# Parameters as rows, late gates of the second block, and state space inputs made ahead in a hybrid decoder block

## The chip, the cores and the metric

The kernel runs on one core of a Trainium2 chip. The metric is the device time of one execution in microseconds (us). Each profile is of one execution. The engines are PE (TensorE, with weight loads listed apart as PEld), DVE (VectorE), ACT (ScalarE), POOL (GpSimd) and SP (SyncE, which issues every DMA here, in program order).

## The reference

One decoder layer for 2048 tokens of width 1024, float32 throughout:

```python
h = _rms(x, norm1_g)
u, q, k, v, qi, ki, wi, gates = split(h @ w_in)           # 512, 512, 64, 64, 256, 64, 4, 2048 columns
# state space: 32 groups of 16 channels and 64 complex states
dt = exp(log_dt); abar = exp((A_re + i A_im) * dt)         # per group and state
b = coef(abar, A) * (B @ u)                                # B: 64 x 16 per group
s = associative_scan(abar, b); y = Re(C @ s) + D_skip * u
y = gelu(y); y_ssm = y * sigmoid(y @ w_glu + b_glu)
# attention: each token takes the 256 visible keys of the highest index score
iscore = sum_heads(relu(qi @ ki^T) * wi); idx = top_k(iscore, 256)
y_att = softmax(q @ k[idx]^T / 8) @ v[idx]                 # 8 heads, one shared k and v
g_ssm, g_att = split(gates)                                # 1024 columns each
merged = sigmoid(g_ssm) * (y_ssm @ w_proj_ssm) + sigmoid(g_att) * (y_att @ w_proj_attn)
x = x + merged @ w_out
x = x + (silu(rms(x) @ w_ffn_gate) * (rms(x) @ w_ffn_up)) @ w_ffn_down   # 2816 hidden columns
```

## The kernel before

All large products run with each float32 operand split in a high and a low part: `mm3` issues three matmuls for each 128 rows of the contraction, so a product of 128 columns by 512 tokens over 1024 rows is 24 matmuls. Every instruction goes through one recording function and therefore carries line 206; a group is told by its tiles.

`phase1` makes the RMS norm, turns `x` into `hT` (high and low), and multiplies it by the columns of `w_in` for u, q, k, v, qi, ki and wi, in tiles `mm`. A step loads pieces of `w_in` into `raw`, DVE and POOL split them into `w`, PE multiplies. Beside this the parameters of the state space branch are computed on DVE. `ssm_params` doesn't run them at once: it fills a list `queue` (with `Later`, which notes a call for later), and `phase1` takes items of it one by one between its own steps. First in the list stand the loads of A_re, A_im, log_dt, D_skip, B_re, B_im, then C_re and C_im, then the arithmetic, then `turns`, which turn C on PE. The half of `hT` for each 1024 tokens is also stored to `hTd`.

Then three generators run side by side, and `Pace` writes their steps into one order when the program is built, by its own estimates of when each engine is free. On the chip this order is fixed for each engine.

- `state`: first `ssm`. Its `prepare` makes, mostly on POOL, the matrices of 8 blocks of 4 groups (powers of abar times B and C: `Gr`, `Er`, `K0`, `M`, `F`, the turned `ET`, the phases `pc`; `N0` is how many columns of the phases are made for all blocks at once). Its `solve` turns the block's inputs U into `Ut`, multiplies them by `ET` (`ee`), runs the recurrence on DVE (`z`, `S`) and multiplies by `M` and `F` into `Y`. `gelu` turns Y to `yT`. All their products use one PSUM bank (`sps`), and an ACT copy empties it each time. Then `glu` multiplies by w_glu (tiles `u<-yp,uw`) and stores `act_d`. When it is through, `gated` is set.
- `attention`: four groups of 4 tiles of 128 tokens. For each, `topk` searches the threshold of the 256th score by counting (on DVE `jkd`, on ACT `jka`, with updates `un`, `tr` on DVE); then `attention` makes the logits (`lg`), the turned probabilities (`pt`, split in `th` and `tl`) and the output (`po`), and stores `att_d`.
- `dense`: first `gates`, 64 products `gps<-hT,gw` (32 column tiles times two runs of 512 tokens; ACT's tanh gives `gsg`, which is stored to `gate_d`). The second half of the tokens (`hf` 1) comes first, from `hT` in SBUF; the first half is loaded back from `hTd`. Then it waits for `gated`, and runs four blocks of 512 tokens in `block`: the two branches' projections (192 matmuls `f<-act,ww`), times the gates, into `mg`; `w_out` (384 matmuls `f<-ww,mg` of 256 columns); norm; FFN up (`f<-h,ww`, then silu and the split `at`) and down (`f<-wd,at`). Block `tb` starts when attention group `tb` is through.

Block 0 loads and splits the weights itself (`raw` to `ww` and `wd`, on DVE, POOL and ACT) and stores the split copies `wc`; the later blocks load them, 1 MB each, through rings of buffers (`Rings`). The list of these items is made in `weights`. At the end of a block the next block's branch inputs `act` are loaded (`load_branch`), 2 MB each.

Of the kernel before, what the change touches and what calls it, by code (L numbers as in the profile page):

```python
# [12 lines left out]
F32 = mybir.dt.float32  # L13
# [22 lines left out]
G = 32  # L36
# [329 lines left out]
class Block:  # L366
    def __init__(self, ctx, tc, a, out):
# [24 lines left out]
        self.bias_d = [d.tile([128, (i + 1) * 128], BF16, name=f"bias{i}") for i in range(NT)]  # L392
        self.gate_d = [[d.tile([128, HALF], F32, name=f"gate{j}_{h}") for h in range(2)] for j in range(2 * KD)]
# [341 lines left out]
    def gates(self, hT, st):  # L735
# [37 lines left out]
        left = [2] * (2 * NG)  # L773
        for q, (n, tg) in enumerate(order):
# [9 lines left out]
            if q in (2 * NG - 2, 2 * NG):  # L784
                parts.extend((q - 2 * NG + 2 >> 1, h, i) for h in range(2) for i in range(2))
# [212 lines left out]
    def attention(self, st, tiles, nP, nT, causal):  # L998
# [6 lines left out]
        tp = self.pool(st, "at", 3 if KL <= 1536 else 2, side="right")  # L1005
# [224 lines left out]
    def ssm_params(self, pr, wk, ps_t, queue):  # L1230
# [3 lines left out]
        dv, sync, cmul = Later(queue, nc.vector), Later(queue, nc.sync), self.cmul  # L1234
        sh = [128, NS]
        A = {}
# [4 lines left out]
        dt = wk.tile(sh, F32, name="dt")  # L1241
        ap = a["log_dt"]
        for g2 in range(2):
            sync.dma_start(dt[g2 * 64:(g2 + 1) * 64],
                              bass.AP(tensor=ap.tensor, offset=ap.offset + g2, ap=[[0, 64], [2, NS]]))
        Ds = pr.tile([32, NS], F32, name="Ds")
        ap = a["D_skip"]
        sync.dma_start(Ds, bass.AP(tensor=ap.tensor, offset=ap.offset, ap=[[1, 32], [32, NS]]))
        B, C, turns = [], [], []
        for n in ("B_re", "B_im"):  # L1250
            t = wk.tile([128, NS, PG], F32, name=n)
            ap = a[n]
            sync.dma_start(t, bass.AP(tensor=ap.tensor, offset=ap.offset,
                                         ap=[[PG, 128], [128 * PG, NS], [1, PG]]))
            B.append(t)
        for n in ("C_re", "C_im"):
# [16 lines left out]
        ar, ai = A["A_re"], A["A_im"]  # L1273
# [55 lines left out]
        u1, u2 = (wk.tile([128, NS, PG], F32, name=f"u{n}") for n in "12")  # L1329
# [5 lines left out]
        dv.tensor_tensor(eye, self.ident[:32, 0:PG], self.ident[:32, PG:2 * PG], op=ALU.add)  # L1335
        queue.extend(turns)
        return m8, ap_r, ap_i, wt, Bb, C, eye, Ds

    def ssm(self, st, params):
# [9 lines left out]
        made = deque()  # L1349
        taken = [0]  # L1350
        NS, N0 = G // 2, 32

        def prepare():
# [8 lines left out]
            dd = wk.tile([32, NS, PG], F32, name="dd")  # L1362
            gp.tensor_tensor(dd, eye[:, None, :].to_broadcast([32, NS, PG]), Ds[:, :, None].to_broadcast([32, NS, PG]),
                             op=ALU.mult)
# [6 lines left out]
            for blk in range(NBLK):  # L1371
# [42 lines left out]
                yield self.pace.idle("POOL", K0)  # L1414
                gp.tensor_tensor(K0[:, :, 0], K0[:, :, 0], dd[:, ss], op=ALU.add)
# [8 lines left out]
                ET = wk.tile([128, 2, SB, 128], F32, name="ET", bufs=2)  # L1424
                for i, E in enumerate((Er, Ei)):
                    yield at("PE", E, psp.free_at("sp"), wk.free_at("ET", 2) if i == 0 else 0.0)
                    ps = psp.tile([128, 512], F32, name="sp")
                    for sp in range(SB):
                        nc.tensor.transpose(ps[:, sp * 128:(sp + 1) * 128],
                                            E[:, sp].rearrange("p t c -> p (t c)"), self.ident)  # L1430
                    nc.scalar.copy(ET[:, i].rearrange("p s n -> p (s n)"), ps[:, :SB * 128])
# [21 lines left out]
                made.append((F2, M, ET, pc))  # L1453
# [6 lines left out]

        def solve(blk):
            s0 = blk * SB
            U = Us.popleft()
            yield lambda: at("PE") if made else NEVER
            F2, M, ET, pc = made.popleft()
            Ut = wk.tile([128, GB, 2, 128], F32, name="Ut")
            for g in range(0, GB, 2):
                yield at("PE", U, psp.free_at("sp"))
                ps = psp.tile([128, 512], F32, name="sp")
                for q in range(4):  # L1470
                    nc.tensor.transpose(ps[:, q * 128:(q + 1) * 128], U[:, q % 2, g + q // 2], self.ident)
                nc.scalar.copy(Ut[:, g:g + 2].rearrange("p g a c -> p (g a c)"), ps)
            if blk + 1 < NBLK:
                Us.append(load(blk + 1))

            ee = wk.tile([128, 2, SB, NCH], F32, name="ee")
            e = [ee[:, i] for i in range(2)]
            for sp in range(SB):
                yield at("PE", ET, Ut, psp.free_at("sp"))
                ps = psp.tile([128, 512], F32, name="sp")  # L1480
                for i in range(2):
                    for g2 in range(2):
                        nc.tensor.matmul(ps[g2 * 64:(g2 + 1) * 64, i * 256:(i + 1) * 256],
# [519 lines left out]
```

## Time and profile before

| | us |
|---|---|
| three runs | 3389.36, 3391.08 (median), 3392.07 |
| profiled execution | 3392.47 |
| its span, first to last instruction | 3390.8 |
| granted TensorE clock, mean | 0.972 |

Where the stages lie in the profiled execution, by the first and last instructions of their tiles on PE (for the searches, on DVE):

| stage | us from the start |
|---|---|
| phase 1 | 0 to 366 |
| gates (`gps`) | 366 to 981 |
| state space (`sp`) | 381 to 782 |
| attention 0 | 518 to 740 |
| search 1 | 758 to about 1155 |
| GLU (`u`) | 799 to 901 |
| block 0, projections from | 990 |
| block 0, `w_out` from | 1065 |
| attention 1 | 1163 to 1383 |
| search 2 | 1414 to 1833, block 1 from 1632 |
| attention 2 | 1833 to 2090 |
| search 3 | 2105 to 2520, block 2 from 2268 |
| attention 3 | 2520 to 2896 |
| block 3, alone | 2924 to the end |

A row of the profile for a group names engine, operation, and the tiles it writes and reads. A wait "PE f <- DVE un" says that PE's next product into `f` was released by DVE's work on `un`. Of several waits the one that ended last is named.

### The profile page before, as it was taken

What the parts mean: (1) busy time and instruction counts of PE and PEld (TensorE: products, weight loads), DVE (VectorE), ACT (ScalarE), POOL (GpSimd) and SP (SyncE); (2) the same over time, 40 slices, a digit from 0 to 9 for tenths busy, and PEclk for the clock granted to TensorE, in tenths of its full rate; (3) what the DMA queues carried; (4) which work ended last, traced back from release to release, by engine and by line L of the source; (5) the groups of instructions that cost most, each with busy time, mean ns of one, the idle gap of its engine ahead of it and who ended that gap; (6) DMA issues with size and microseconds to landing.
All of it is one profiled execution on the core that took longest, in us unless ns stands there. A gap on an engine that the chain in (4) does not pass through costs nothing. (4 is left out here: it accounts for less than half of the span.)

```text
span 3390.8 us, 44218 instructions
## 1 busy us (share of the span) xinstructions
PE 3179.1 (94%) x16292; PEld 2687.4 (79%) x16292; DVE 2118.4 (62%) x4540; ACT 1277.2 (38%) x2210; POOL 622.4 (18%) x620
## 2 busy tenths in 40 slices
PE   6999999899878999988889999999999999899999
PEld 5889777677767888876788888878888888698887
DVE  5565595655687767689686675867776666322223
ACT  3141444445552444355412443666124443010000
POOL 3323666522233212134100000000000000000000
PEclk8999999999989999999999999999999999999999
DMA  4834423434458766656845324376472332755554
GB/s 135 249 119 116 132 77 121 153 123 142 130 174 293 271 210 231 238 175 236 310 152 218 146 105 165 123 259 229 166 271 99 114 133 103 271 193 201 204 199 161
DMA packets 321527, 605.67 MB, mean 179 GB/s; under 512 B 52896, under 2 KB 205216, under 8 KB 290592
## 3 DMA queue, kind: packets, MB, share of 16 engines
q1 hardware_dynamic: 321312, 602.86, 51.1%
q8 instruction: 128, 2.10, 0.2%
q14 instruction: 87, 0.71, 0.1%
HBM read 434.71 MB, written 166.89 MB: 177 GB/s over the span
## 5 line engine op out<-in xcount | busy, mean ns | idle before, releaser
L206 PE MATMUL f<-h,ww 128*128 128x512 f32 (+1 forms) x4416 | 1015.0, 384 | 1.4 <-DVE h L206 1.1
L206 PEld LDWEIGHTS f<-h,ww 128*128 128x128 f32 x4416 | 800.6, 190 | 156.4 <-DVE h L206 1.9
L206 PE MATMUL f<-wd,at 128*128 128x512 f32 x2112 | 521.1, 399 | 42.8 <-DVE un L206 16.0
L206 PEld LDWEIGHTS f<-wd,at 128*128 128x128 f32 x2112 | 398.5, 192 | 133.3 <-DVE x L206 13.6
L206 PE MATMUL gps<-hT,gw 128*128 128x512 f32 x1536 | 386.5, 402 | 5.2 <-ACT gsg L206 3.7
L206 ACT ACTIVATE jka<-S,tr 128x1536 bf16<-128x1536 f32 (+5 forms) x217 | 305.6, 1408 | 193.6 <-DVE tr L206 119.2
L206 PEld LDWEIGHTS gps<-hT,gw 128*128 128x128 f32 x1536 | 287.7, 192 | 70.0 <-ACT gsg L206 6.4
L206 DVE TENSOR_TENSOR x<-f,x 128x512 f32<-128x512 f32 x352 | 236.4, 687 | 103.2 <-PE f L206 102.5
L206 PE MATMUL mm<-w,hT 128*128 128x512 f32 (+1 forms) x1152 | 281.5, 402 | 7.2 <-DVE hT L206 7.0
L206 DVE TENSOR_TENSOR tl<-pt,th 128x512 fp32r<-128x512 f32 (+1 forms) x288 | 184.2, 658 | 135.9 <-ACT th L206 135.1
L206 PEld LDWEIGHTS mm<-w,hT 128*128 128x128 f32 x1152 | 241.8, 241 | 32.6 <-DVE hT L206 8.7
L206 DVE SCALAR_TENSOR_TENSOR t<-t,f 128x512 f32<-128x512 f32 (+1 forms) x125 | 83.5, 668 | 278.5 <-PE f L206 238.0
L206 ACT CAST th<-pt 128x512 fp32r<-128x512 f32 (+1 forms) x288 | 155.8, 563 | 234.1 <-PE pt L206 230.3
L206 PE MATMUL f<-act,ww 128*128 128x512 f32 x768 | 189.9, 408 | 29.7 <-POOL ww L206 9.1
L206 PEld LDWEIGHTS f<-act,ww 128*128 128x128 f32 x768 | 149.2, 197 | 70.3 <-POOL ww L206 13.3
L206 PE MATMUL f<-ww,mg 128*128 128x256 f32 x1536 | 190.4, 287 | 10.8 <-ACT ww L206 4.5
L206 PEld LDWEIGHTS f<-ww,mg 128*128 128x128 f32 x1536 | 188.7, 195 | 12.9 <-ACT ww L206 5.0
L206 ACT ACTIVATE P<-P,m 128x1024 f32<-128x1024 f32 (+7 forms) x192 | 172.3, 900 | 54.5 <-DVE m L206 54.4
L206 POOL TENSOR_TENSOR g<-g,g 128x512 f32<-128x512 f32 x31 | 39.8, 1285 | 813.3 <-DVE g L206 793.5
L206 PE MATMUL lg<-kk,q 128*128 128x512 f32 (+1 forms) x640 | 183.7, 388 | 1.1 <-DMA kk<-kk 1.1
L206 ACT ACTIVATE t<-f 128x512 f32<-128x512 f32 (+1 forms) x92 | 53.0, 576 | 332.9 <-PE f L206 332.7
L206 ACT CAST at<-t 128x512 fp32r<-128x512 f32 (+1 forms) x92 | 55.3, 601 | 324.1 <-DVE t L206 324.1
(359 smaller groups left out, 4492.2 us busy)
## 6 DMA issues: line engine op xcount, KB each, us to landing
ww<-wc SPq DMA_DIRECT2D x180, 1024.0 KB, 4.9
wd<-wc SPq DMA_DIRECT2D x66, 1024.0 KB, 8.3
wc<-ww SPq DMA_DIRECT2D x60, 1024.0 KB, 7.7
raw<-in_w_in_dram SPq DMA_DIRECT2D x104, 256.0 KB, 3.4
wc<-wd SPq DMA_DIRECT2D x22, 1024.0 KB, 7.6
x<-in_x_dram SPq DMA_DIRECT2D x32, 512.0 KB, 5.1
gate<-gsg SPq DMA_DIRECT2D x64, 256.0 KB, 2.2
g<-gate SPq DMA_DIRECT2D x64, 256.0 KB, 5.0
```

Of the source, the lines that this page charges most:

```text
L206: return f(*args, **kw)
```

## The change

It has three parts.

1. `ssm_params` loads A_re, A_im, D_skip and log_dt as 16 rows each, of contiguous runs (128, 128, 32 and 2 numbers), instead of number by number into columns, and turns them on PE in one bank (`columns`). Each load of B is cut in four, and these eight stand between the steps of the arithmetic, one after every sixth.
2. The gates of block 1's tokens (16 of the 64 products: first half of the tokens, second run of 512) leave `gates`. The split weights for them are stored as `gw_d`, 16 tiles of 1 MB. At the end of block 0 `load_tokens` loads `hT` of these tokens into the buffers of `act`; `block` makes the 16 products first, then loads the two branches into the same buffers, the attention's first, and takes the branches in that order.
3. In `ssm` the inputs' part of `solve` becomes a generator `enter`, up to one block ahead. Both halves of `ET` take one bank and one copy; `ee` one copy for both parts; `Y` one bank and one copy for each 128 channels, with both pairs of groups in it. The skip D is added on DVE. `N0` is 16, not 32. Apart from these, `th` and `tl` in attention 0 have two buffers, not three.

```diff
@@ gates
-        order = [(n, tg) for n in range(2 * NG) for tg in range(2)]
-        order[2 * NG - 4:2 * NG + 4] = [(NG + n, tg) for n0 in (-2, 0) for tg in range(2) for n in (n0, n0 + 1)]
+        order = [(n, tg) for n in range(NG) for tg in range(2)] + [(NG + n, 0) for n in range(NG)]
+        order[2 * NG - 4:2 * NG] = [(n, tg) for tg in range(2) for n in (NG - 2, NG - 1)]
...
+            if n >= NG:
+                nc.sync.dma_start(self.gw_d[ct], w.rearrange("p z k c -> p z (k c)").bitcast(F32))
@@ ssm_params
-        for n in ("A_re", "A_im"):
-            A[n] = wk.tile(sh, F32, name=n)
-            ap = a[n]
-            sync.dma_start(A[n], bass.AP(tensor=ap.tensor, offset=ap.offset, ap=[[1, 128], [128, NS]]))
...
+        for z, n, m in ((rows[0], "A_re", 128), (rows[1], "A_im", 128), (d32, "D_skip", 32), (d2, "log_dt", 2)):
+            sync.dma_start(z, bass.AP(tensor=a[n].tensor, offset=a[n].offset, ap=[[m, NS], [1, m]]))
...
+            for i, z in enumerate(rows):
+                nc.tensor.transpose(ps[:, i * NS:(i + 1) * NS], z, self.ident[:NS, :NS])
+            nc.tensor.transpose(ps[:32, 3 * NS:4 * NS], d32, self.ident[:NS, :NS])
+            nc.scalar.copy(A.rearrange("p a s -> p (a s)"), ps[:, :3 * NS])
...
-            sync.dma_start(t, bass.AP(tensor=ap.tensor, offset=ap.offset,
-                                         ap=[[PG, 128], [128 * PG, NS], [1, PG]]))
+            for s0 in range(0, NS, 4):
+                sync.dma_start(t[:, s0:s0 + 4], bass.AP(tensor=ap.tensor, offset=ap.offset + s0 * 128 * PG,
+                                                        ap=[[PG, 128], [128 * PG, 4], [1, PG]]))
...
+        queue.extend(head)
+        queue.extend(loads.popleft() for _ in range(24))
+        queue.append(columns)
+        for i, step in enumerate(steps):
+            queue.append(step)
+            if i % 6 == 5 and loads:
+                queue.append(loads.popleft())
@@ ssm
+        def enter():
+            U = load(0)
+            for blk in range(NBLK):
+                yield lambda: at("PE") if turned and len(entered) < 1 else NEVER
...
-                for i in range(2):
-                    nc.scalar.copy(e[i][:, sp], ps[:, i * 256:(i + 1) * 256])
+                    nc.scalar.copy(ee[:, :, sp], ps.rearrange("p (i c) -> p i c", i=2))
...
-        return self.pace.among([apply(), prepare()])
+        return self.pace.among([apply(), enter(), prepare()])
@@ block
+            if tb in self.late:
+                b0 = 1
...
+                    order = list(range(KD))
+                    last = 3
+                    for ct in range(2 * KD - last):
+                        w = ld.get("w")
+                        yield ready(w, *hg)
+                        ps = bank()
+                        yield from products(ps, w, order)
+                        ld.drop("w")
+                        gated(ct, ps)
+                    order = [*range(KD // 2, KD), *range(KD // 2)]
+                    banks = []
+                    for i in range(last):
+                        w = ld.get("w", i)
+                        yield ready(w)
+                        banks.append(bank(False))
+                        yield from products(banks[i], w, order[:KD // 2])
+                    self.act = [None, self.load_branch(bigp, 1, tb)]
+                    for i in range(last):
+                        w = ld.get("w")
+                        yield from products(banks[i], w, order[KD // 2:])
+                        ld.drop("w")
+                        gated(2 * KD - last + i, banks[i])
+                    self.act[0] = self.load_branch(bigp, 0, tb)
```

How the order of instructions changes is shown at three places. The first is SP's queue in phase 1, where the parameters are loaded; `u_577` and `u_578` are the tiles of the rows. Before:

```order
L206 DMA raw<-in_w_in_dram 128x512 x3
L206 DMA A_re<-in_A_re_dram 128x16x1
L206 DMA A_im<-in_A_im_dram 128x16x1
L206 DMA dt<-in_log_dt_dram 64x16x1 x2
L206 DMA Ds<-in_D_skip_dram 32x16x1
L206 DMA B_re<-in_B_re_dram 128x16x16
L206 DMA B_im<-in_B_im_dram 128x16x16
L206 DMA C_re_568<-in_C_re_dram 16x2x64
L206 DMA raw<-in_w_in_dram 128x512 x3
```

Seven loads of parameters and one of C stand between two groups of weight loads. SP's queue at the same place after:

```order
L206 DMA raw<-in_w_in_dram 128x512 x3
L206 DMA u_577<-in_A_re_dram 16x128
L206 DMA u_577<-in_A_im_dram 16x128
L206 DMA u_578<-in_D_skip_dram 16x32
L206 DMA u_578<-in_log_dt_dram 16x2
L206 DMA C_re_584<-in_C_re_dram 16x2x64 x4
L206 DMA raw<-in_w_in_dram 128x512 x3
```

Four loads of rows and four of C stand there, and none of B. The second place is PE at the end of the gates, with the GLU's products `u` and the first products of block 0. Before:

```order
L206 MATMUL gps<-hT,gw 128x512 x24
L206 MATMUL u<-yp,uw_7369 128x256 x12
L206 MATMUL u<-yp,uw_7374 128x256 x12
L206 MATMUL gps<-hT,gw 128x512 x6
L206 MATMUL u<-yp,uw_7416 128x256 x12
L206 MATMUL u<-yp,uw_7443 128x256 x12
L206 MATMUL gps<-hT,gw 128x512 x330
L206 MATMUL f<-act_9327,ww 128x512 x24
```

330 matmuls of gates stand between the GLU's last products and block 0. PE's order at the same place after, with the products `tps` of search 1 among them:

```order
L206 MATMUL gps<-hT,gw 128x512 x24
L206 MATMUL u<-yp,uw_7375 128x256 x12
L206 MATMUL u<-yp,uw_7402 128x256 x12
L206 MATMUL tps<-kis,qi 128x512 x4
L206 MATMUL u<-yp,uw_7327 128x256 x12
L206 MATMUL u<-yp,uw_7332 128x256 x12
L206 MATMUL tps<-kis,qi 128x512 x4
L206 MATMUL tps<-kis,qi 128x256 x8
L206 MATMUL u<-yp,uw_7375 128x256 x12
L206 MATMUL u<-yp,uw_7402 128x256 x12
L206 MATMUL u<-yp,uw_7327 128x256 x12
L206 MATMUL u<-yp,uw_7332 128x256 x12
```

The last gates stand ahead of the last ten GLU groups here (two of them follow these rows), and block 0's first product `f` follows the GLU. The third place is PE from block 0's last products to block 1's first. Before:

```order
L206 MATMUL f<-h_9802,ww 128x512 x12
L206 MATMUL f<-h_9803,ww 128x512 x12
L206 MATMUL f<-wd,at 128x512 x96
L206 MATMUL f<-act_14451,ww 128x512 x24
L206 MATMUL f<-act_14456,ww 128x512 x24
```

Block 1's projections follow block 0's last products. PE's order at the same place after, from the end of the late gates (`hg` are the tokens' tiles; 13 products of 24 matmuls stand ahead of these rows, and ahead of them the last 66 of `f<-wd,at`):

```order
L206 MATMUL f<-hg_13749,ww 128x512 x12
L206 MATMUL f<-hg_13752,ww 128x512 x48
L206 MATMUL f<-hg_13749,ww 128x512 x36
L206 MATMUL f<-act_14727,ww 128x512 x24
L206 MATMUL f<-act_14807,ww 128x512 x24
```

The 384 matmuls of the late gates stand between the last product of block 0 and the projections of block 1; the last three products are taken half by half.

More of the change, by code (lines that the diff above doesn't have):

```diff
@@ L1272, in ssm_params @@
             C.append(t)
-        ar, ai = A["A_re"], A["A_im"]
+        ar, ai = A[:, 0], A[:, 1]
         edt, _ = self.exp_parts(dv, dt, wk, sh, "ed")
@@ L1335, in ssm_params @@
         dv.tensor_tensor(eye, self.ident[:32, 0:PG], self.ident[:32, PG:2 * PG], op=ALU.add)
+        loads.extend(late)
+        queue.extend(head)
[5 more added lines that the diff above has]
+                queue.append(loads.popleft())
+        assert not loads and len(steps) > 7 * 16
         queue.extend(turns)
@@ L1413, in prepare @@
                 nc.scalar.copy(K0.rearrange("p s t c -> p (s t c)"), ps[:32, :SB * 128])
-                yield self.pace.idle("POOL", K0)
-                gp.tensor_tensor(K0[:, :, 0], K0[:, :, 0], dd[:, ss], op=ALU.add)
+                yield at("DVE", K0)
+                for sp in range(SB):
+                    dv.scalar_tensor_tensor(K0[:, sp, 0], eye, Ds[:, s0 + sp:s0 + sp + 1], K0[:, sp, 0], op0=ALU.mult,
+                                            op1=ALU.add)
                 M = Ms[blk % 2]
@@ L1461, in solve @@
         def solve(blk):
             s0 = blk * SB
[L1463 to L1472, printed above, removed]
@@ L1473, in solve @@
-            if blk + 1 < NBLK:
-                Us.append(load(blk + 1))
-            ee = wk.tile([128, 2, SB, NCH], F32, name="ee")
-            e = [ee[:, i] for i in range(2)]
-            for sp in range(SB):
-                yield at("PE", ET, Ut, psp.free_at("sp"))
-                ps = psp.tile([128, 512], F32, name="sp")
-                for i in range(2):
-                    for g2 in range(2):
-                        nc.tensor.matmul(ps[g2 * 64:(g2 + 1) * 64, i * 256:(i + 1) * 256],
-                                         ET[:, i, sp, g2 * 64:(g2 + 1) * 64],
-                                         Ut[:, sp * 2 + g2].rearrange("p a c -> p (a c)"), start=True, stop=True)
-                for i in range(2):
-                    nc.scalar.copy(e[i][:, sp], ps[:, i * 256:(i + 1) * 256])
+            yield lambda: at("PE") if made and entered else NEVER
@@ L1664, in weights @@
         copies = [self.dram.tile([128, 2, 1024], F32, name=f"wc{i}") for i in range(len(items))]
-        return [(kind, parts, copy, tb > 0) for tb in range(NB) for (kind, parts), copy in zip(items, copies)]
+        return [z for tb in range(NB) for z in
+                [("w", None, copy, True) for copy in self.gw_d if tb in self.late] +
+                [(kind, parts, copy, tb > 0) for (kind, parts), copy in zip(items, copies)]]
     def load_branch(self, bigp, br, tb):
@@ L1672, in load_branch, with load_tokens @@
         return z
+    def load_tokens(self, bigp, tb):
+        hg = []
+        for i in range(2):
+            ks = slice(i * KD // 2, (i + 1) * KD // 2)
+            hg.append(bigp.tile([128, 2, KD // 2, TB], F32R, name=f"hg{i}", tag=f"act{i}"))
+            for z in range(2):
+                self.nc.sync.dma_start(hg[i][:, z].bitcast(F32), self.hT_d[:, z, ks, tb * TB:(tb + 1) * TB])
+        return hg
     def block(self, tb, bigp, ld, nps, nd):
@@ L1918, in block @@
             if tb + 1 < NB:
-                self.act = [self.load_branch(bigp, br, tb + 1) for br in range(1 + (self.attended >= 4 * (tb + 2)))]
+                if tb + 1 in self.late:
+                    self.act = self.load_tokens(bigp, tb + 1)
+                else:
+                    self.act = [self.load_branch(bigp, br, tb + 1)
+                                for br in range(1 + (self.attended >= 4 * (tb + 2)))]
             yield from down(pairs.popleft(), False)
```

133 lines of the change are left out of this document (90 added, 43 removed).

## The prediction

> **What bounds the kernel now.** I read the page's busy times first, then a table of windows cut at the stages, then the waits of TensorE (PE) inside each stage, and last the timelines at the waits that the change touches.
>
> ```profile
> PE 3179.1 (94%) x16292; PEld 2687.4 (79%) x16292; DVE 2118.4 (62%) x4540; ACT 1277.2 (38%) x2210; POOL 622.4 (18%) x620
> ```
>
> PE is busy for 3179.1 of a span of 3390.8 us and no other engine is above 62%. The change keeps the matmuls (the late gates are the same products in another place), so only the 211.7 us in which PE idles, and stretches at a low clock, can move. Where they lie, by stage (columns: length; busy time of PE, PEld, DVE, ACT, POOL; granted clock; DMA share; GB/s):
>
> ```profile
> 366.00:758.00 392.00, 360.98 (x1796) 285.45 (x1797) 256.56 (x586) 185.17 (x413) 230.04 (x348) 0.94 0.38 118
> 758.00:1163.00 405.00, 352.43 (x1888) 298.77 (x1887) 282.31 (x664) 188.34 (x318) 104.45 (x70) 0.95 0.58 191
> 1163.00:1414.00 251.00, 249.80 (x1324) 211.47 (x1323) 166.53 (x324) 108.54 (x188) 45.92 (x20) 1.00 0.66 229
> 1414.00:1834.00 420.00, 379.30 (x1837) 317.50 (x1836) 332.63 (x676) 171.39 (x226) 91.90 (x48) 0.95 0.64 231
> 1834.00:2105.00 271.00, 270.12 (x1542) 233.19 (x1540) 181.36 (x399) 121.98 (x254) 0.00 (x0) 1.00 0.36 130
> 2105.00:2520.00 415.00, 393.70 (x1932) 333.00 (x1932) 319.31 (x688) 194.35 (x222) 15.19 (x16) 0.97 0.56 206
> ```
>
> The stages are: state space beside attention 0 (31 us idle), search 1 with the gates, the GLU and the start of block 0 (53), attention 1 (1), search 2 (41), attention 2 (1), search 3 (21). PE idles while a search loads VectorE (DVE), hardly ever in an attention stage.
>
> **Part 1, parameters as rows.** The rows are the one wait of PE between 69 and 92 us, SyncE's (SP's) queue, DVE's and PE's first work after it, and a window behind it.
>
> ```profile
> PE tp L206 <- DVE hT L206: 22.2, 1, 22.2
> ```
> ```profile
> 56.80 0.42 SPq L206 DMA_DIRECT2D A_re<-in_A_re_dram  x1
> 57.28 3.56 SPq L206 DMA_DIRECT2D A_im<-in_A_im_dram  x1
> 60.88 2.57 SPq L206 DMA_DIRECT2D dt<-in_log_dt_dram  x2
> 63.49 3.12 SPq L206 DMA_DIRECT2D Ds<-in_D_skip_dram  x1
> 66.66 4.80 SPq L206 DMA_DIRECT2D B_re<-in_B_re_dram  x1
> 71.50 12.86 SPq L206 DMA_DIRECT2D B_im<-in_B_im_dram  x1
> ...
> 85.81 1.31 SPq L206 DMA_DIRECT2D raw<-in_w_in_dram  x3
> 87.18 3.98 SPq L206 DMA_DIRECT2D C_re<-in_C_re_dram  x8
> ```
> ```profile
> 88.70 0.43 DVE L206 CAST w<-raw 128x512 fp32r<-128x512 f32 x1 [23.31 <-DMA raw<-in_w_in_dram]
> ...
> 91.74 1.97 PE L206 MATMUL tp<-ident,q 128*128 128x128 f32 x8 [22.15 <-DVE hT L206]
> ```
> ```profile
> 91.00:96.00 5.00, 4.26 (x14) 3.76 (x15) 3.58 (x5) 0.10 (x1) 2.98 (x3) 0.50 0.72 221
> ```
>
> Seven element-wise loads stand on SP from 56.80 to 84.36 us. The weight load `raw` stands behind them, DVE idles 23.31 us for it, and PE 22.15 us for DVE; behind that the granted clock is 0.50. In the new order eight short DMAs (four rows, four of C) stand ahead of the same `raw`. Eight such loads of C took 3.98 us, so 4 us stand there instead of 27.6: the queue is shorter by 23.6 us, more than the wait. I take the whole 22.2 us and about 2 us of the half clock (5 us at 0.50 lose 2.5): **−24**, bounds 0 (if the loads of the weights stand behind something else) and −25. Four turns on PE and four copies on ACT are added while PE waits or runs full; like `tp` turns they take under a us, so 0.
>
> The loads of B are cut in eight, not re-formed: their runs stay 64 bytes long. In the rows they hold SP for 4.80 + 12.86 = 17.66 us, so 2.2 us a piece, issued one between each six steps of DVE, with `raw` loads between them. A wait of 2.2 us spread over products of 24 matmuls can be hidden: 0, bounds 0 and +17.7. The Trainium skill ("DMA: Bandwidth & Descriptors", sections Specifications and Rules for kernel authors) says that an innermost run with stride costs one descriptor per element, and that runs under 512 bytes don't reach line rate. By its measure A, log_dt and D are mended wholly and B not at all, and the sum would be +17.7 worse; the trace agrees as far as the loads with 4-byte and 64-byte runs alone hold SP for more than 2 us.
>
> **Part 2, the state space branch.** It has one PSUM bank (`sps`), so each product waits for the copy of the one before. The waits of PE between 366 and 758 us, and ACT's copies of Y:
>
> ```profile
> PE sp L206 <- DVE z L206: 10.0, 3, 5.7
> PE sp L206 <- ACT Y L206: 8.0, 4, 2.7
> PE sp L206 <- ACT Ut L206: 4.5, 2, 4.3
> PE sp L206 <- ACT ee L206: 4.1, 2, 3.8
> PE sp L206 <- DVE S L206: 1.9, 2, 1.6
> ```
> ```profile
> L206 ACT COPY Y<-sp 128x256 f32<-128x256 f32 x32 | 11.8, 370 | 39.8 <-PE sp L206 37.3 <-issue 2.5
> ```
>
> The sums are 28.5 us in the five first rows. Y goes from four turns of the bank per block to two, with copies twice as wide: of its 8.0 us I take −5. `Ut` and `ee` are made up to a block ahead, when nothing waits for them: of 8.6 us half, −5 with rounding. `z` and `S` are the recurrence itself, 0. Sum **−10**. Bounds: −28.5, if `z` waited because its inputs were late; +8.6, if the new generator holds the one bank when `solve` wants it. The skip's move from POOL to DVE is 16 additions of 32x16 on a DVE with 135 us idle in that stage: 0. Two buffers for `th` and `tl` instead of three in attention 0: of the stage's 31.0 us of idle time all but 2.5 stand in the five rows, so 0, bounds 0 and +2.5 (that rest once more).
>
> **Part 3, the late gates.** Sixteen gate products (384 matmuls) leave search 1 and stand in front of block 1, in search 2. Their length, and what block 0 and block 1 lose under a search:
>
> ```profile
> 990.00:1065.00 75.00, 55.76 (x193) 40.32 (x192) 55.03 (x116) 17.77 (x26) 31.53 (x19) 0.86 0.86 298
> 1065.00:1163.00 98.00, 90.97 (x622) 85.17 (x623) 71.57 (x121) 34.33 (x49) 22.22 (x12) 0.95 0.74 268
> ...
> 3100.00:3200.00 100.00, 100.00 (x443) 82.81 (x442) 24.56 (x36) 7.30 (x12) 0.00 (x0) 1.00 0.52 198
> ```
>
> Undisturbed, a matmul takes 100/443 = 0.226 us, so the late gates are 87 us. Search 1 ends near 1155 us by the marks; its DVE work is not moved, so 87 us more of block 0 now run beside it. Block 0 lost 7.03 of 98 us (7.2%) in its second window: 87 × 7.2% = **+6**. The last GLU groups lose their company too; the waits of this stretch:
>
> ```profile
> PE f L206 <- DMA act<-act: 8.9, 1, 8.9
> PE u L206 <- ACT t L206: 7.9, 7, 2.2
> PE u L206 <- DVE yp L206: 3.8, 5, 1.0
> ```
>
> Twelve GLU waits cost 11.7 us now, 0.98 us each, beside gates; ten groups stand behind the last gate in the new order. Between 0 and +9.8 for them I take **+5**. The 8.9 us for the first branch's load stay, since it follows the GLU in both orders. Bounds of these two terms: 0 and +77 (the rival below, and 9.8).
>
> Search 2 gains what it had lost, as far as gates, which ask DVE for nothing, replace FFN work. PE's waits there:
>
> ```profile
> PE f L206 <- DVE un L206: 10.7, 4, 4.9
> PE f L206 <- DVE x L206: 9.4, 4, 4.7
> ...
> PE f L206 <- DVE t L206: 2.5, 1, 2.5
> ```
>
> These 22.6 us are waits for a DVE behind in its queue. The gates cover 87 of the search's 218 us (1414 to 1632), and block 1's products then meet the rest: half, −11. The branches are loaded late, into the tiles that hold the tokens: the load of the attention's share goes while 36 matmuls (8.1 us) run, and such loads land in some 9 us, so +2 for both. Together **−9**, bounds −22.6 and +9. Storing and loading the split weights is 32 MB more; a load of 1 MB has 87/16 = 5.4 us, or 193 GB/s, and the row of 990:1065 shows 298 GB/s: 0, bounds 0 and +9 (one such load late).
>
> The end: attention 3 now stands further ahead of block 3, whose start waited here (from 2888 to 2960 us):
>
> ```profile
> PE f L206 <- DMA wd<-wc: 6.3, 2, 5.4
> PE f L206 <- DMA act<-att: 3.5, 3, 1.9
> ```
>
> The second row goes, and the first stays: **−4**, bounds −9.8 and 0.
>
> **Sum.** −24 −10 +6 +5 −9 −4 = −36. The profiled execution took 3392.5 us, so 3356.5; it lies 1.4 us above the median of the runs, 3391.1, so **3355**. Less than 0.2% (6.8 us) I call no change.
>
> **The rivals.**
> - *Block 0 under a whole search (slower).* Its first products, 193 matmuls, took 75 us and should take 43.6: 42% lost, with splits on POOL and ACT beside a search on DVE. In the new order block 0 has 165 + 87 = 252 us beside search 1, of which 177 follow the first window. At 42% these lose 74 us, against 7 now: +67 in place of +6, or 3416 us. For it: the splits of weights go on through block 0. Against it: the second window, also beside the search, lost only 7.2%. It decides from a loss of 28% on (177 × 28% = 50 = 7 + 6 + 36).
> - *The stall comes back at B.* Its 17.7 us of SP time fall on loads that PE waits for: 3373 us. For it: 12.86 us for one load of 64-byte runs. Against it: the pieces stand between weight loads that are issued ahead. The rule of the Trainium skill cited above ("DMA: Bandwidth & Descriptors", Rules for kernel authors) speaks for this one.
> - *More is gained than I take.* `z` was late for its inputs, so that all 28.5 us of the branch go, and all 22.6 of search 2: 19 and 13 us more, 3323 us. For it: DVE busy only 65% beside `z`. Against it: the recurrence is a chain, and search 2 ends when DVE does.
> - *The change does less than it says*, as the bank is the bound and not the turns: neither fuller banks nor gates in another place count, and only part 1 does: 3391 − 24 = 3367 us, inside the first case.
>
> **How the numbers follow.** My forecast has 0.50, with a band of its own from 3335 to 3376 (half the way to the bounds of the branch and of search 2, 16 us down and 18 up, and some 3 for the GLU); the larger gain 0.20; the return of the stall 0.16; block 0 under the search 0.14. The range from 3312 to 3392 takes in the first three; its low end is that of the larger gain with the end's and the GLU's bounds, 11 us on. Out of it are most of the slower case and little else. Faster by over 0.2%: 0.50 + 0.20 + nearly all of 0.16, less a little of each for the unknown: 0.80; no change 0.10 (the slower case at about 28% and a stall with small gains); slower 0.10.
>
> **What would show it.** Right: between 55 and 100 us no load on SP but B above 1 us, and no wait of PE above 5 us; waits on `Y`, `Ut` and `ee` under 8 us together; PE idle in the stretch from the GLU's end to search 1's end near 7%; in front of block 1 a stretch of 384 `f` products with hardly a wait, and then waits on `un` and `x` of half their size. Wrong: a wait on `raw` or `w` behind a piece of B; waits of `f` on `ww` from POOL or ACT of 40 us or more in block 0; a wait of 5 us or more on `act` in front of block 1; a new wait of `sp` on a bank held by `Ut`.

## The result and the profile after

The changed kernel takes 3430.7 us (median of 4, 3427.9 to 3431.8) against 3391.6 us before: ratio 1.011, 95% interval 1.0095 to 1.0126, 38 us slower. The forecast was 3355 us, 36 us faster. Of the rivals, block 0 under a whole search (3416 us) had the right sign and place.

The page's first line for the changed kernel shows the same matmuls in a longer span (3429.3 us):

```profile
PE 3186.1 (93%) x16296; PEld 2689.7 (78%) x16296; DVE 2140.7 (62%) x4554; ACT 1270.9 (37%) x2176; POOL 644.5 (19%) x652
```

The windows of the changed kernel at its own stages (columns as before): state space and attention 0; block 0's projections, its `w_out` and norm, its FFN, all three beside search 1; search 2 up to block 0's end; the late gates.

```profile
352.00:757.00 405.00, 365.92 (x1843) 288.71 (x1844) 282.44 (x613) 190.60 (x391) 235.20 (x380) 0.96 0.41 127
...
900.00:976.00 76.00, 55.90 (x193) 41.46 (x193) 54.90 (x122) 33.14 (x53) 33.75 (x19) 0.84 0.85 295
976.00:1062.00 86.00, 53.81 (x401) 52.20 (x401) 75.47 (x176) 42.33 (x71) 45.16 (x22) 0.78 0.52 180
1062.00:1234.00 172.00, 149.15 (x664) 122.00 (x664) 144.70 (x252) 43.20 (x67) 65.05 (x29) 0.93 0.68 238
...
1483.00:1579.00 96.00, 86.00 (x361) 68.78 (x362) 75.76 (x130) 46.05 (x55) 14.54 (x9) 0.93 0.63 229
1579.00:1671.00 92.00, 87.36 (x385) 71.69 (x383) 76.72 (x273) 79.37 (x105) 0.00 (x0) 1.00 0.73 242
```

Block 0 now spends 334 us beside search 1, and PE is busy for 259 of them; in `w_out` and norm it is busy for 54 of 86. The late gates run as meant: their 384 matmuls stand in the last window, of 92 us, which has one more.

To add up losses, idle time and low clock together, I take for each stretch its length less its matmuls at the spacing that they have where nothing is waited for (0.227 us for 512 columns). In us:

| stretch | before | changed | part 1 alone | part 3 alone | part 2 alone | 1 and 3 |
|---|---|---|---|---|---|---|
| to the first gate | 66.0 | 51.2 | 52.3 | 66.6 | 66.2 | 50.8 |
| to the end of attention 0 | 53.8 | 58.9 | 54.7 | 64.4 | 39.1 | 65.6 |
| to block 0's first product | 34.9 | 41.5 | 39.0 | 36.6 | 55.3 | 36.0 |
| block 0 (with attention 1) | 95.7 | 132.3 | 98.2 | 124.9 | 123.0 | 125.9 |
| late gates, block 1's projections | 0.0 | 15.5 | 0.1 | 2.0 | 15.1 | 2.8 |
| from there to block 3 | 86.9 | 80.4 | 80.7 | 77.3 | 86.1 | 76.8 |
| block 3 | 8.4 | 4.1 | 7.9 | 2.5 | 3.1 | 2.1 |
| all | 345.7 | 383.9 | 332.9 | 374.3 | 387.9 | 360.0 |

The four columns on the right are the first experiments. The profiled execution of parts 1 and 3 took 3407.8 us, 8 above the median of its runs, so that its column is some 8 us high. What the changed kernel gains in phase 1 (15) and in the last rows (11) it loses twice over in block 0 (37) and in front of block 1's `w_out` (15).

### The profile page after: what moved, and what is told of

Same layout as the page of the kernel before. It is cut to its first block, busy times and chain, and to the rows that moved or that the text cites. A ratio compares the mean times of both kernels' runs of the same rounds, so it can differ in the third digit from the quotient of the medians.

```text
span 3429.3 us, 44303 instructions
## 1 busy us (share of the span) xinstructions
PE 3186.1 (93%) x16296; PEld 2689.7 (78%) x16296; DVE 2140.7 (62%) x4554; ACT 1270.9 (37%) x2176; POOL 644.5 (19%) x652
## 5 line engine op out<-in xcount | busy, mean ns | idle before, releaser
L206 ACT ACTIVATE jka<-S,tr 128x1536 bf16<-128x1536 f32 (+6 forms) x217 | 305.4, 1407 | 195.3 <-DVE tr L206 112.6
L206 PE MATMUL gps<-hT,gw 128*128 128x512 f32 x1152 | 295.0, 405 | 3.3 <-ACT gw L206 2.0
L206 PEld LDWEIGHTS gps<-hT,gw 128*128 128x128 f32 x1152 | 216.0, 193 | 51.5 <-issue 3.5
L206 ACT CAST at<-t 128x512 fp32r<-128x512 f32 (+1 forms) x92 | 55.3, 601 | 359.6 <-DVE t L206 359.1
```

What stands on the lines that cost most here:

```text
L206: return f(*args, **kw)
```

## The experiments

All ratios are to the kernel before, run on the same chip.

| kernel | median, us | ratio, 95% interval |
|---|---|---|
| part 1 alone | 3380.3 | 0.9955 (0.9942 to 0.9969) |
| part 3 alone | 3419.6 | 1.0076 (1.0062 to 1.0089) |
| parts 1 and 3 | 3400.0 | 1.0023 (1.0013 to 1.0032) |
| part 2 alone | 3433.5 | 1.0119 (1.0105 to 1.0133) |
| before, no splits | 3346.2 | 0.9863 (0.9847 to 0.9880) |
| changed, no splits | 3374.7 | 0.9948 (0.9933 to 0.9963) |
| part 3, no splits | 3347.9 | 0.9867 (0.9853 to 0.9882) |
| changed, block 0's splits without POOL | 3401.0 | 1.0027 (1.0014 to 1.0040) |
| part 1, the same | 3372.5 | 0.9945 (0.9933 to 0.9958) |
| parts 1 and 3, the same | 3379.5 | 0.9956 (0.9944 to 0.9969) |
| changed, half the late gates | 3437.2 | 1.0130 (1.0117 to 1.0143) |
| part 2, gates inside block 0 | 3439.2 | 1.0132 (1.0117 to 1.0146) |
| part 1, splits without POOL, idle POOL operations | 3438.8 | 1.0135 (1.0122 to 1.0149) |
| part 3 without the lead | 3392.9 | 1.0001 (0.9990 to 1.0011) |
| part 1, no split on POOL after phase 1 | 3363.3 | 0.9909 (0.9896 to 0.9923) |
| changed, no branch loads in block 1 | 3422.2 | 1.0086 (1.0069 to 1.0102) |
| the fastest, with part 3 without lead | 3387.6 | 0.9987 (0.9978 to 0.9996) |
| changed, no split on POOL after phase 1 | 3409.5 | 1.0057 (1.0045 to 1.0070) |

**Each part alone.** My first theory after the result was that the late gates do all the harm (lost cover), and that parts 1 and 3 do none; the rival, that parts 1 and 3 spoil the order. Each of the four kernels takes whole functions from one of the two versions.

Part 1 alone (`ssm_params` of the changed kernel in the kernel before):

> The kernel before with part 1 alone (the parameters as rows, B in eight pieces). Lost cover (the late gates alone make the changed kernel slow): phase 1 is 15 us shorter, as in the changed kernel (352 us to the first gate instead of 366), and nothing else changes: 3376 us. The prediction's step: 24 us less, 3367. Rival (a shorter phase 1 moves the order that is planned behind it, and the gain is given back): 3386 to 3396.

Part 3 alone (`ssm` and `attention`):

> The kernel before with part 3 alone (inputs of the state space branch made ahead, fuller banks, skip on DVE, two buffers for th and tl). Lost cover: the waits only change their names, as in the changed kernel, where the stretch from the first gate to the end of attention 0 lost 5 us more than before: 3391 to 3398 us. The prediction's step: 10 us less, 3381. Rival (this part spoils the order of search 1 and block 0): 3410 or more.

Parts 1 and 3 (the changed kernel with the old `gates`, `weights`, `block`):

> The changed kernel without part 2: all 64 gate products in the gates' own stage again, parts 1 and 3 kept. Lost cover: block 0's loss beside search 1 falls from 104 us back to about 44, and the time to 3391 - 15 + 5 = 3381 us. Rival (parts 1 and 3 brought block 0 under the search in a bad order): it stays above 3410.

Part 2 alone:

> The kernel before with part 2 alone (the 16 gate products of block 1's tokens late). Lost cover: the whole loss comes with it: +61 for block 0 and +7 for the GLU, -24 in search 2, +15 in front of block 1, -10 at the end, so +49: 3440 us. Rival (the loss needs parts 1 and 3): 3385 to 3400.

Part 1 gains 15 us, as in the changed kernel. Part 2 alone costs 40 and part 3 alone 26, so both theories are half right: neither is harmless, and together (−15 + 26 + 40 = 51 against 38) the parts overlap by 13. In the table both raise the loss of block 0 by 27 to 29 us. With part 3 the attention's chain runs ahead of block 0: search 2 stands beside 302 us of block 0 instead of 218.

**No splits.** What sets block 0 apart from the later blocks is that it splits its weights.

```diff
-        copies = [self.dram.tile([128, 2, 1024], F32, name=f"wc{i}") for i in range(len(items))]
+        copies = [self.hT_d[:, :, i % KD] for i in range(len(items))]
...
-        (kind, parts, copy, tb > 0)
+        (kind, parts, copy, True)
```

The edit also takes away the loads of the raw weights and the stores of the copies; these runs don't separate them from the splits.

> The kernel before, but no block splits weights: every block loads its 1 MB weight tiles ready made (from the store of hT, so with wrong numbers), no raw weights of the blocks are loaded and no copies stored. Theory (block 0's loss beside a search is the splitting of its weights): block 0 lost 84 us of 391 beside searches, block 1 lost 8% of its own; at 8% block 0 loses 31: 53 us less, 3338 us. Rival (it is the search's order on VectorE, and splits hide): 10 us less or nothing, 3381 to 3391.

> The changed kernel with the same cut (weight tiles ready made, no splits). Theory of the splits: block 0 lost 120 us of 430, at 8% it loses 34: 86 us less, 3344 us, so that the changed kernel and the one before are within 10 us of each other. Rival (the late gates take cover away whether weights are split or not): it stays some 38 us above the kernel before with the same cut.

> The kernel before with part 3 alone, and the same cut (weight tiles ready made, no splits). Theory of the splits: the 26 us that part 3 costs are block 0 pushed further under search 2, so they go: 108 us of loss become 35, 3346 us, within 10 us of the kernel before with the same cut. Rival (part 3 costs by itself, in the state space branch): 20 us or more above it.

Block 0's loss falls from 95.7 to 43.6 us (before), from 124.9 to 36.0 (part 3) and from 132.3 to 51.2 (changed). Part 3 then costs nothing against the kernel before: its price was block 0's splitting (with its loads and stores), put under search 2. The late gates still cost, and no less than with splits: less the 15 us of part 1, the changed kernel should take 3331, and takes 3375. So the splits explain where block 0 loses its time, but not the price of the late gates. Two windows of the kernel before without splits, then three of the changed one without splits, show where: the first two of each are block 0 beside search 1 and beside search 2, the last one of the changed kernel is block 1's projections.

```profile
994.00:1129.00 135.00, 123.93 (x754) 110.40 (x754) 82.91 (x204) 25.98 (x46) 15.99 (x14) 0.96 0.69 243
1321.00:1580.00 259.00, 251.56 (x1098) 206.32 (x1098) 207.26 (x558) 138.08 (x177) 1.59 (x4) 0.98 0.53 191
```
```profile
906.00:1129.00 223.00, 207.50 (x1107) 179.34 (x1107) 157.25 (x505) 91.82 (x157) 15.99 (x14) 0.95 0.63 219
1330.00:1503.00 173.00, 164.94 (x712) 134.63 (x713) 141.81 (x385) 119.09 (x150) 1.59 (x4) 0.97 0.55 198
1597.00:1667.00 70.00, 51.33 (x196) 39.45 (x196) 27.52 (x42) 7.52 (x12) 8.97 (x7) 0.87 0.86 311
```

Beside search 2 nothing was left to gain (7 of 259 us idle), and block 1's projections, after the late gates, are idle for 19 of 70 us.

**GpSimd.** In the changed kernel's trace some of DVE's operations beside the splits take ten times their usual time. DVE's updates of the search (`tr`), and POOL's operations at the same time:

```profile
1015.55 1.87 DVE L206 SCALAR_TENSOR_TENSOR tr<-un,tr 128x2 int32<-128x2 int32 x1
1017.53 2.38 DVE L206 SCALAR_TENSOR_TENSOR tr<-un,tr 128x1 int32<-128x1 int32 x1
1020.00 1.75 DVE L206 SCALAR_TENSOR_TENSOR tr<-un,tr 128x1 int32<-128x1 int32 x1
1025.29 0.16 DVE L206 SCALAR_TENSOR_TENSOR tr<-un,tr 128x1 int32<-128x1 int32 x1
```
```profile
1015.52 1.89 POOL L206 TENSOR_TENSOR ww<-raw,zeros 128x1024 fp32r<-128x1024 f32 x1 [2.31 <-PE f L206]
1017.49 2.40 POOL L206 TENSOR_TENSOR ww<-raw,ww 128x1024 fp32r<-128x1024 f32 x1
1019.85 1.89 POOL L206 TENSOR_TENSOR ww<-raw,zeros 128x1024 fp32r<-128x1024 f32 x1
```

An update of one number per partition takes 0.16 us, and 1.75 to 2.38 us when a POOL operation is under way: it ends when that one ends. The Trainium skill states it ("SBUF — State Buffer", section Who interferes with whom): VectorE and GpSimd share a pair of ports, a VectorE instruction with two SBUF inputs contends with a GpSimd instruction that reads SBUF, and the one that comes second blocks until the first is through. The trace agrees. I counted for every shape of DVE operation what it took beyond its shortest tenth while it overlapped one of POOL. Beside block 0 and the two searches that is 67 us before (21 and 46), 82 in the changed kernel, 92 with parts 1 and 3, and about 2 us in operations that overlapped none.

```diff
 class Rings(Loader):
+    SPLIT = (("ACT",), ("DVE",))
...
-        eng = p.spare(hi, ("POOL", "DVE", "ACT"))
+        eng = p.spare(hi, self.SPLIT[0])
...
-        p.spare(lo).tensor_tensor(lo, raw, hi.bitcast(F32), op=ALU.subtract)
+        p.spare(lo, self.SPLIT[1]).tensor_tensor(lo, raw, hi.bitcast(F32), op=ALU.subtract)
```

> The changed kernel, with block 0's weights split by ScalarE (high part) and VectorE (low part) alone, nothing on GpSimd. Theory (operations of VectorE that overlap one of GpSimd are drawn out, 76 us in all in block 0's stretch beside search 1, 92 with the neighbouring stages): VectorE loses these 76 us and takes some 33 subtractions of 1.2 us instead, 40 us: 30 us less, 3400 us. Rival (VectorE is full there, and GpSimd only helped): 40 us more, 3470.

> The kernel before with part 1, and block 0's weights split without GpSimd (high part on ScalarE, low part on VectorE). GpSimd's splits draw VectorE out in this order too: by the overlap counted in the trace of before 26 us (758 to 990), 21 (990 to 1163) and 46 (1414 to 1632). If that is what costs (as in the changed kernel, where the same edit gave 30 us): 3380 - 30 = 3350 us. Rival (the changed kernel gained because it is full beside search 1, and this one is not): 3370 to 3380.

> The changed kernel without late gates, and block 0's weights split without GpSimd. If part 3 costs its 26 us by pushing more of block 0's splitting under search 2, with GpSimd's drawn-out VectorE, most of that goes: 3400 - 30 - 15 = 3355 us, near the kernel with part 1 and the same splits (within 10 us). Rival (part 3 costs as much with other splits): 20 us or more above that one.

The edit gains 28 us in the changed kernel, about as expected, and 23 with parts 1 and 3, half of what was expected. With part 1 alone it gains only 3 by the ratios (the intervals overlap), as its rival said. DVE's busy time over block 0 falls there all the same, from 489 to 439 us, but PE idles as long (58 of 645 us, then 56 of 644): beside search 1 it waits 11.9 us for DVE's `ww` where it had waited 11.9 for POOL's, and beside search 2 for the high parts that ACT alone now makes:

```profile
PE f L206 <- ACT wd L206: 18.2, 4, 7.1
```

Part 3's price falls from 23 us (parts 1 and 3 against part 1) to 4. The group `tr` for one number: beside search 1 in the changed kernel, the same stretch with splits without POOL, and the changed kernel's late gates, where POOL is idle.

```profile
L206 DVE SCALAR_TENSOR_TENSOR tr<-un,tr 128x1 int32<-128x1 int32 x58 | 35.8, 618 | 2.0
```
```profile
L206 DVE SCALAR_TENSOR_TENSOR tr<-un,tr 128x1 int32<-128x1 int32 x59 | 10.5, 179 | 2.0
```
```profile
L206 DVE SCALAR_TENSOR_TENSOR tr<-un,tr 128x1 int32<-128x1 int32 x47 | 7.5, 159 | 1.6
```

Does POOL cost by its presence, or as a slow splitter? The next kernel adds operations on POOL that do no work, and leaves the order of DVE's instructions as it was:

```diff
         super().split()
+        self.b.pace.gpsimd.eng.tensor_tensor(self.d1, self.d0, self.b.zeros[:, :1].to_broadcast([128, 1024]), op=ALU.add)
```

> The kernel with part 1 and splits without GpSimd, with one GpSimd operation on two private tiles (128x1024 plus zeros, about 2 us) added beside each of block 0's splits; it does nothing for the result, and VectorE's order of instructions is the same. GpSimd draws VectorE out: VectorE's search operations are some 60 us longer in sum again beside block 0, and the time rises from 3372 by 20 to 40 us, to 3392 to 3412. Rival (GpSimd cost only as a slow splitter that PE waits for): 3368 to 3377.

It costs 64 us by the ratios, above the range expected. The windows of block 0 beside search 1 without these operations, and then with them, and the group of them in the second:

```profile
974.00:1150.00 176.00, 146.44 (x801) 126.98 (x802) 112.08 (x242) 50.09 (x74) 16.01 (x14) 0.87 0.75 268
```
```profile
978.00:1194.00 216.00, 149.41 (x799) 129.00 (x800) 167.07 (x248) 50.70 (x74) 107.32 (x57) 0.81 0.61 216
```
```profile
L334 POOL TENSOR_TENSOR dummy<-dummy,zeros 128x1024 f32<-128x1024 f32 x43 | 93.4, 2172 | 2.7
```

The same 800 matmuls take 40 us more; DVE is busy for 55 us more with the same work. A part may be POOL's own few operations behind the added ones (14 in this window), which this run doesn't separate.

Last, the gates' and the GLU's weights are split without POOL too:

```diff
-    SPLIT = (("POOL", "DVE", "ACT"), ("POOL", "DVE"))
+    SPLIT = (("ACT", "DVE"), ("DVE",))
```

> The kernel with part 1 and no GpSimd in the splits of block 0 (3372 us), and none in the splits of the gates' and the GLU's weights either. GpSimd draws VectorE out: 26 us of that lay between 758 and 990 us, where PE lost 35 us; a quarter of it comes back, 3362 to 3368 us. Rival (VectorE has room there): 3370 to 3376.

This is the fastest version, 0.9909: 31 us faster than the kernel before.

**The lead of part 3.**

```diff
-                yield lambda: at("PE") if turned and len(entered) < 1 else NEVER
+                yield lambda: at("PE") if turned and made and len(entered) < 1 else NEVER
```

> The kernel before with part 3, but the inputs of a block are turned and multiplied only once its matrices are made and the block before has taken its own (no lead); fuller banks, skip on VectorE and the buffers of th and tl stay. If the lead is what ends the state space branch 22 us earlier and attention 0 38 us later (and so puts more of block 0 under search 2): back to 3391 to 3398 us. Rival (fuller banks or the skip on VectorE): it stays at 3412 to 3420.

Without the lead part 3 costs nothing, so the lead is what costs the 26 us in that kernel. Search 2 beside block 0, with the lead and then without it:

```profile
1372.00:1674.00 302.00, 258.52 (x1050) 206.82 (x1049) 270.89 (x497) 146.71 (x185) 123.85 (x55) 0.92 0.64 226
```
```profile
1418.00:1635.00 217.00, 191.58 (x780) 152.49 (x778) 193.09 (x362) 119.18 (x149) 77.67 (x36) 0.92 0.66 232
```

The share of idle time is alike (14 and 12%), but the lead puts 85 us more of block 0 there.

> Part 1, part 3 without the inputs' lead, no late gates, no GpSimd in any split of weights. If the lead was all that part 3 changed in time: the time of the kernel with part 1 and the same splits, 3363 us, within 5. Rival (the banks' fewer turns count once VectorE is free): 3350 to 3357.

That failed: 24 us above the fastest version. Its loss is some 23 us higher by the end of attention 0, and about as much higher at the end of the run. PE's waits on the recurrence there, in the fastest version and then with part 3 without lead:

```profile
PE sp L206 <- DVE S L206: 13.7, 6, 5.2
```
```profile
PE sp L206 <- DVE S L206: 27.1, 10, 6.9
```

So what is left of part 3 without the lead (fuller banks, the skip on DVE, `N0`, two buffers) costs nothing beside the old splits and some 24 us beside the new ones. Which of these edits does it, or whether it is the planner's order, is open.

**The late gates.**

```diff
+        order = [(n, tg) for n, tg in order if n < NG + 8 or tg == 0]
...
-                    for ct in range(2 * KD - last):
+                    for ct in range(8, 2 * KD - last):
```

> The changed kernel with 8 of the 16 gate products late, and 8 back beside the GLU. Cover (each gate product taken from search 1 costs its share): half of the 31 us that the late gates add to parts 1 and 3 (3431 against 3400): 3415 us. Rival (the loss is one accident of the order, the 25.8 us wait of PE for the norm of block 0): either all of it or nothing, 3400 or 3431.

Half the gates cost as much as all. So the price doesn't go by the number of gates; the time is the rival's, but not for its reason, since the wait for the norm is 12.6 us there and not 25.8. The other kernel makes the 16 products in block 0, after `w_out` (the block of code of part 2 stands there, the tokens loaded after the projections):

> The kernel before with part 2 alone, but the 16 products stand in block 0, between w_out and the norm, instead of in front of block 1 (so the junk tile of the norm is its own). Cover: 87 us of matmuls that need no VectorE stand in search 1 again, where PE waited 25.8 us for the norm; that wait and the 15 us in front of block 1 go, the 24 us gained in search 2 are given back, and the GLU stays uncovered: 3433 - 26 - 15 + 24 - 10 = 3406 us. Rival (loading the tokens and weights there costs as much as it covers): 3425 or more.

It is no faster than part 2 alone, as its rival said. Block 0's loss beside search 1 and beside search 2 (us), for twelve of the versions, shows a trade:

| | beside search 1 | beside search 2 | both |
|---|---|---|---|
| before | 43.8 | 42.5 | 86 |
| part 2 alone | 95.0 | 15.7 | 111 |
| parts 1 and 3 | 43.4 | 66.5 | 110 |
| changed | 104.4 | 15.6 | 120 |
| half the late gates | 70.1 | 46.3 | 116 |
| gates inside block 0 | 66.6 | 65.7 | 132 |
| part 1, splits without POOL | 49.3 | 39.4 | 89 |
| parts 1 and 3, splits without POOL | 38.7 | 39.3 | 78 |
| changed, the same | 85.7 | 4.8 | 91 |
| before, no splits | 19.2 | 11.7 | 31 |
| part 3, no splits | 16.9 | 11.3 | 28 |
| changed, no splits | 27.2 | 12.6 | 40 |

In the four pairs in like company all 16 late gates in front of block 1 add 25 us (part 2 alone), 10 (changed), 13 (splits without POOL) and 12 (no splits) to the sum. What makes up this sum is not shown further. Most of the rest of their price lies in front of block 1's `w_out`, where SP's queue in the changed kernel shows the loads of the branches, and weights behind them:

```profile
1650.42 0.32 SPq L206 DMA_DIRECT2D gate<-lg  x1
1658.29 2.54 SPq L206 DMA_DIRECT2D act<-att  x4
1661.01 1.03 SPq L206 DMA_DIRECT2D ww<-wc  x1
...
1672.92 2.54 SPq L206 DMA_DIRECT2D act<-act  x4
1675.51 2.87 SPq L206 DMA_DIRECT2D g<-gate  x4
1684.45 0.32 SPq L206 DMA_DIRECT2D ww<-wc  x1
```

SP stands still for 7 us until the tokens' tile is free, and the weights `ww` are issued behind that. PE's waits from the late gates to `w_out`:

```profile
PE f L206 <- DMA ww<-wc: 8.4, 2, 4.8
PE f L206 <- DMA act<-act: 2.2, 4, 1.0
```

```diff
-                    self.act = [None, self.load_branch(bigp, 1, tb)]
+                    self.act = [hg[0], hg[1]]
...
-                    self.act[0] = self.load_branch(bigp, 0, tb)
```

> The changed kernel without the loads of block 1's branches: its projections read the tokens' tiles again (wrong numbers, the same matmuls). If the 15 us that PE waits in front of block 1 come from these loads and from weight loads that stand behind them on SP: 3431 - 13 = 3418 us. Rival (the weights are late by themselves, after 16 MB of stored gate weights): 3428 to 3433.

It gains 8 us of the 13 expected; the loss of that stretch falls from 15.5 to 8.4, and 5.6 us of waits on `ww` stay. The run takes away 4 MB of loads with their place in the queue, so it doesn't tell the one from the other. Last, the changed kernel with no split on POOL after phase 1:

> The changed kernel with no GpSimd in any split of weights. If the late gates only trade idle time of search 2 for idle time of search 1 and add 13 us in front of block 1: 3363 + 7 for part 3 + 21 = 3391 us. Rival (with VectorE as planned the gates are worth their move): 3363 or less.

It takes 3409, above both expectations, and 46 us (50 by the ratios) above the fastest version: the late gates and part 3 don't pay with these splits either.

## Why the prediction was wrong, point by point

The forecast was −36 us and the result +38. Of the 74 us between them, part 1 makes 9 (−24 against −15), the state space branch 36 (−10 against +26) and the late gates 42 (−2 against +40), less the 13 by which the parts overlap. The branch and the gates failed at the same place: they were priced with 6 us and with nothing for what they do to block 0, whose loss beside the searches grew from 86 to 120 us.

**Part 1, −24: right in mechanism, too large.** It gave −15. The queue is as forecast, with `raw` 5.9 us behind the load of A_re, against 29.0 before. SP's queue in the changed kernel:

```profile
55.86 0.42 SPq L206 DMA_DIRECT2D u<-in_A_re_dram  x1
...
58.05 3.18 SPq L206 DMA_DIRECT2D C_re<-in_C_re_dram  x4
61.77 3.03 SPq L206 DMA_DIRECT2D raw<-in_w_in_dram  x3
```

The wait of 22.2 us is gone, and B cost nothing that PE shows: that rival falls, and with it what I let the rule on short runs weigh. What the prediction cites of the Trainium skill ("DMA: Bandwidth & Descriptors", Specifications and Rules for kernel authors) was also misapplied: of the new rows only A's reach its 512 bytes (D's have 128, log_dt's 8), and its rule on stride doesn't touch B, whose runs are whole. The four loads of rows hold SP for 0.41 to 0.46 us each, whatever their length. But some 7 us came back as new waits in phase 1 (`tp` for `u` 3.9, `mm` for `w` 2.1, `tp` for C 0.9). The 3.9 us are the new step itself: PE's turns of the rows stand behind ACT's copy into `u`, and ACT makes it last of several copies. I had put the turns and copies at 0, and taken the whole wait as gain.

**Part 2 of the prediction, the state space branch (part 3 of the change), −10: wrong in sign.** Alone it costs 26 us. PE's waits in the changed kernel's stretch from the first gate to attention 0's end:

```profile
PE sp L206 <- DVE S L206: 13.6, 6, 6.3
PE sp L206 <- ACT yT L206: 5.3, 4, 2.9
PE sp L206 <- POOL Gr L206: 4.2, 1, 4.2
...
PE sp L206 <- ACT Ut L206: 0.8, 1, 0.8
PE sp L206 <- ACT Y L206: 0.6, 2, 0.4
```

The waits on `Y` and `Ut` went as forecast. But `S` and `yT` took their place (1.9 to 13.6 and 0.5 to 5.3), so that they seem to have been time in which PE would have waited for the recurrence anyway. The larger fault is that I priced the edit only in its own stage: the lead moved 85 us of block 0 under search 2, and without the lead, or without block 0's splits, the 26 us are gone.

**Part 3 of the prediction, late gates, −2: the failed step is the 7.2% for block 0 beside search 1.** In the prediction's terms the +6 was +61 in the changed kernel (43.8 to 104.4) and +51 with part 2 alone; the GLU's +5 was about +7 (the whole stretch up to block 0); search 2's −9 was −27 there and +15.5 in front of block 1; and the end's −4 was −4, by the wait that I had named. That search 2's term came out near −9 in sum is luck: its waits on `un` and `x` went altogether, where I had taken half, and the late weights in front of block 1 made up for it.

I took the loss of 7.2% from the 98 us before attention 1. By the measure of the tables, with the low clock, that window lost 12%. It was no window with little to split: 30 operations of the splits start in it, against 16 in the window before, but POOL made only 6 of the 30. After its first window in the changed kernel, block 0 lost 72 of 258 us, 28%, and POOL made 45 of the 68 such operations there. The search ended 71 us later (1163 to 1234), which I had held fixed though block 0's work shares DVE with it. Without any splits 27 of the 104 us remain, and with splits on ACT and DVE alone 86, so POOL is a part of it only. The single wait to notice is that for the norm:

```profile
PE f L206 <- DVE ss L206: 25.8, 1, 25.8
PE f L206 <- POOL ww L206: 14.9, 9, 2.4
PE f L206 <- DMA act<-act: 10.6, 1, 10.6
PE f L206 <- ACT ww L206: 6.8, 4, 3.8
```

It is 25.0 us with part 2 alone and 12.6 with half the gates. In the changed kernel with splits without POOL it falls to 4.5, and the waits for ACT's splits grow from 6.8 to 22.5:

```profile
PE f L206 <- ACT ww L206: 22.5, 9, 5.6
...
PE f L206 <- DVE ss L206: 4.5, 1, 4.5
```

**The 32 MB at nothing and the late branches at +2.** PE never waits for the stored gate weights. The stretch up to block 1's `w_out` lost 15.5 us instead; without the loads of the branches 7 to 8 of them go. The 5.6 us of waits on `ww` that stay may be a price of the 32 MB, which no run separates.

**The chances.** I gave the slower side 0.10, and its rival, block 0 under a whole search, 0.14. That its price came out is in part luck: the 74 us of loss after the first window came as 72, but as 28% of 258 us and not as 42% of 177, and its sign, 40 us of waits on `ww` from POOL or ACT in block 0, stayed at 22. The profile of before held the evidence: block 0 lost 86 of 391 us beside searches, block 1 only 30 of 364.

## What to carry to other kernels

Price a moved piece of work by what the stretch that it leaves loses under the same company, not by the mildest window near it; where two chains share one engine in a fixed order, as the search and block 0 share DVE here, moving work between two stages mostly traded idle time. Look for operations that take ten times their usual time before believing an engine's busy share: taking the splits off GpSimd and loading the parameters as rows gave 31 us, more than any reordering here.

## What the runs showed of the hardware

- A DVE operation with two SBUF inputs that meets a POOL operation lasts until that one ends: 0.16 us became 1.75 to 2.38 us. Some with one tensor input are drawn out too: `un<-cnt` on 128x2 took 1.46 us on average where it overlapped a POOL operation beside search 1 of the changed kernel, and 0.17 elsewhere there, but on 128x1 0.14 and 0.15. Operations with one input in PSUM didn't change: `x<-f,x` took 682 ns on average beside search 1 and 686 beside attention 1 in the changed kernel.
- POOL operations without any use, 82 of 2.2 us on average, cost 64 us of the whole time.
- Cutting the loads of B, with runs of 64 bytes, in eight pieces between other loads took them off PE's path altogether. The first piece holds SP for 2.5 us and the others for 0.4 to 0.8, 6.4 in all against 17.7 for the two whole loads. What a load holds SP for went by its place as well as by its runs: in the kernel before A_re, number by number but the first of the seven, held it for 0.42 us, and in the changed kernel single loads of C held it for 2.5 to 3.2 us between 102 and 124 us, where eight of them took 3.96 us at 65 us.
